# A two-layer encoder step on one core: the second layer's up product in seven block products for 26 of its 32 units, with the residual stored to DRAM and loaded again in between

## The chip, the cores and the metric

The kernel runs on one core of a Trainium2 chip. The metric is the device time of one execution in microseconds; smaller is better. The kernel before took 2478.04 us, the median of 3 runs (2475.95 to 2481.3).

## What is computed

The reference is one inference step of a two-layer encoder on 1024 prompt rows and 32 sample rows (T = 1056 columns when the rows are laid along the free axis), width D = 1024, fp32. Layer 0 is an mLSTM mixer and an MLP, layer 1 is a chunk-band attention and an MLP. Only the MLP of layer 1 matters here:

```python
u = x * (1 + sc2) + sh2                       # x: after the first LayerNorm of the layer
f = jnp.square(jax.nn.relu(u @ w_up)) @ w_down   # 1024 -> 4096 -> 1024
x = layer_norm(ALPHA * x + (1 + g2) * f, ln_g, ln_b)
```

Results must hold fp32 accuracy, so every fp32 operand of these products is split into a high part (a cast to fp32r) and a low part (the rest), and each product is three matmuls: high x high, high x low, low x high.

## The kernel before, in words

**Tiles.** Feature rows lie on the 128 partitions, the 1056 columns on the free axis. `QN` = 264 columns are a quarter; two quarters are a pair. Pair 1 (columns 528 to 1055) goes first (`tp0` = 1), pair 0 second (`tp1` = 0). The 4096 hidden rows are 16 blocks `pb` of 256 rows. A *unit* is one block for one pair, so there are 32. The modulated input lies in `u2[pair]` (high and low, 8 row blocks of 128), and the residual x in one tile `ACC` (128 x 8 x 1056 fp32) from the pool `acc1` (L1705), into which the down product adds.

**Up product** (`mlp7`, L1124). `up_tile` (through `up_mm` and `proj`, L118 to L120) makes one 128 x 264 tile with 8 row blocks x 3 = 24 matmuls; a unit has four of them, 96 matmuls. ScalarE applies relu from PSUM (L1159) and the square (L1162) in a tile `H`. VectorE then forms sums and differences of the four quadrants (L1164 to L1166), splits them into `HL`, and one store puts the seven forms of the unit into DRAM (`hd`, L1170). Blocks 14 and 15 (`NW` = 14 and up) go through `up_plain` (L1180) and are stored as plain high and low parts (`hpl`, L1191). The weights of a block come in two loads of 512 KB (`up_weights`, `wblock`, `split` at L89 on ScalarE and L90 on VectorE).

**Down product.** Blocks 0 to 13 lie in four groups (`GRP`: 3, 4, 3, 4 blocks). For each group and each of four column blocks of `w_down`, `unit` (L1268) makes a product in Strassen's manner with seven block products (`PRODS`) where eight stand in the plain one. `forms` (L1222) makes the seven forms of the weights: 7 splits, each a ScalarE cast and a VectorE subtraction, and 4 VectorE sums or differences. Each of a unit's products is kg x 3 matmuls (kg blocks in the group) for each pair and is added to `ACC` by VectorE (L986). `Rooms` (L1098) hands out free space in SBUF, and `fill` (L1261) loads the wanted forms from `hd` into it (`fx`, L1117), pair 1 before pair 0, in the order of `PRODS`. The first column block of the first group goes first for pair 1 and then for pair 0. Last come blocks 14 and 15 as a plain product (`hs` from `hpl`).

**Order of the work.** PE's order in the down product is written out by hand (`manual_schedule`). All other instructions of an engine stand in a fixed list that the scheduler makes when the kernel is built; each engine runs its list in order and stops at the first instruction whose inputs are not there. All loads and stores are issued by one queue, SP's, in the order of its list. `Flow` spreads long tasks such as the LayerNorm (`norm`, L846) over the product's ticks: `L.ready(i)` ends the LayerNorm of the i-th column block (order 2, 1, 0). When the up product begins, the LayerNorm of blocks 1 and 0 is still running beside it.

**Buffers.** Raw weights go through a ring `raw` of 3 tiles, split weights and forms through a ring `wc` of 6, `H` has 3 tiles and `HL` one.

Of the kernel before, what the change touches and what calls it, by code (L numbers as in the profile page):

```python
# [75 lines left out]
def trunk_kernel(ctx: ExitStack, tc: tile.TileContext, a, o):  # L76
# [61 lines left out]
    xsp = [dr.tile([P, KC, T], F32, name=f"xsp{l}") for l in range(2)]  # L138
# [954 lines left out]
    B11, B22, B21, T1, T3, T2, T4 = range(7)  # L1093
# [30 lines left out]
    def mlp7(L):  # L1124
# [5 lines left out]


        l, mm = L.l, L.alloc
        w_dn = a["w_down"][l]
        hd = [[dr.tile([7, P, kg, 2, QN], F32, name=f"hd{l}_{g}_{tp}") for tp in range(2)]
              for g, (_, kg) in enumerate(GRP)]
        hpl = dr.tile([4, P, 2, T], F32, name=f"hpl{l}")
        hh_cm = tc.tile_pool(name=f"hh{l}", bufs=1, reuse_waits="tile")
# [13 lines left out]

        def up_tile(pb, f, q):

            tp = q // 2
            ps = up_mm(pb, f, q)
            if (pb, tp) not in hts:
                hts[pb, tp] = [hhp.tile([P, 8, QN], F32, tag="H", name=f"H{l}_{pb}_{tp}", bufs=3), 0]
            H = hts[pb, tp][0]
            nc.scalar.activation(H[:, ((0, 1), (3, 2))[f][q % 2]], ps, AF.Relu)  # L1159
            hts[pb, tp][1] += 1  # L1160
            if hts[pb, tp][1] == 4:
                nc.scalar.activation(H[:, 0:4], H[:, 0:4], AF.Square)  # L1162
                HL = hhp.tile([P, 7, 2, QN], F32R, tag="HL", name=f"HL{l}_{pb}_{tp}", bufs=1)
                nc.vector.tensor_sub(H[:, 4:6], H[:, 1:3], H[:, 0:2])  # L1164
                nc.vector.tensor_sub(H[:, 6], H[:, 2], H[:, 4])
                nc.vector.tensor_sub(H[:, 7], H[:, 3], H[:, 6])  # L1166
                split(HL[:, 0, 0], HL[:, 0, 1], H[:, 0])
                split(HL[:, 1:, 0], HL[:, 1:, 1], H[:, 2:])
                g = [i for i, (p0, kg) in enumerate(GRP) if p0 <= pb][-1]
                nc.sync.dma_start(hd[g][tp][:, :, pb - GRP[g][0]].rearrange("f p l t -> p f (l t)"),  # L1170
                                  HL.bitcast(F32).rearrange("p f l t -> p f (l t)"))
            flow.tick(QN / 96)
# [7 lines left out]
        def up_plain(pb, tp):  # L1180
            for f in range(2):
                r = tmp_t([P, 2, QN], f"hr{l}_{pb}_{f}_{tp}")
                for i in range(2):
                    nc.scalar.activation(r[:, i], up_mm(pb, f, 2 * tp + i), AF.Relu)
                    flow.tick(QN / 96)
                nc.scalar.activation(r, r, AF.Square)
                name = f"hl{l}_{pb}_{f}_{tp}"
                hl = hlp.tile([P, 2, 2, QN], F32R, tag="hl", name=name, bufs=2) if pb == NPB - 1 else \
                    ring.tile([P, 2, 2, QN], F32R, tag="raw", name=name, bufs=3)
                split(hl[:, 0], hl[:, 1], r)  # L1190
                nc.sync.dma_start(hpl[2 * (pb - NW) + f, :, :, 2 * tp * QN:2 * (tp + 1) * QN],  # L1191
                                  hl.bitcast(F32).rearrange("p l q t -> p l (q t)"))

        tp0, tp1 = L.pairs

        for i in range(2):
            L.ready(i)
            for pb in range(3):
                for f in range(2):
                    up_tile(pb, f, L.quarters[i])  # L1200
                if i and pb < 2:
                    del wups[pb]
                    up_w(3 + pb)
        up_unit(3, tp0)
        up_unit(4, tp0)
        L.ready(2)
        for pb in (2, 3, 4, 0, 1):
            up_unit(pb, tp1)
        for pb in range(5, NW):
            for tp in L.pairs:  # L1210
                up_unit(pb, tp)
        for pb in range(NW, NPB):
            up_w(pb)
        hh_cm.__exit__(None, None, None)
        f4_cm = tc.tile_pool(name=f"f4{l}", bufs=1, reuse_waits="tile")
        f4p = f4_cm.__enter__()
        f4 = [f4p.tile([P, KG, 2, QN], F32R, tag=f"f4{i}", name=f"fx_4{i}_{l}") for i in range(4)]
        hl_cm = tc.tile_pool(name=f"hl{l}", bufs=1, reuse_waits="tile")
        hlp = hl_cm.__enter__()


        def forms(g, m, nm):  # L1222

            raw = []
            p0, kg = GRP[g]
            for i in range(2):
                r = raw_tile([P, kg, 256], f"rdn_{nm}_{i}")
                nc.sync.dma_start(r, w_dn[p0 * 256:(p0 + kg) * 256, m * 256:(m + 1) * 256].rearrange(
                    "(k s p) c -> s p k c", s=2, p=P)[i])
# [24 lines left out]
            w = pair()  # L1254
            split(w[:, 0, 0], w[:, 0, 1], a22)
            yield out

        fx, nfx = {}, {}
        want = []
# [31 lines left out]
        order_f = [f for _, f, _, _, _ in PRODS]  # L1291
        preps, got = {}, {}
        units = [(g, m, [(tp0,), (tp1,)] if g + m == 0 else [(tp0, tp1)]) for g in range(len(GRP)) for m in range(4)]

        def prep(i):
            if i < len(units):
                preps[i] = forms(*units[i][:2], f"{l}_{i}")
                next(preps[i])
        for t in f4:
            rooms.add(t)  # L1300
        want += [(tp, f) for tp in L.pairs for f in order_f]
        fill(0, fx)
        for tp in L.pairs:
            up_plain(NW, tp)
        prep(0)
        up_plain(NW + 1, tp0)
# [3 lines left out]
        for t in L.rooms(tp0):  # L1310
            rooms.add(t)
        fill(0, fx)
        up_plain(NW + 1, tp1)
        for t in L.rooms(tp1):
            rooms.add(t)
        fill(0, fx)
        hl_cm.__exit__(None, None, None)
        f5_cm = tc.tile_pool(name=f"f5{l}", bufs=1, reuse_waits="tile")
        rooms.add(f5_cm.__enter__().tile([P, KG, 2, QN], F32R, name=f"fx_5_{l}"))
        fill(0, fx)  # L1320
        with tc.manual_schedule(engines={mybir.EngineType.PE}):
            for i, (g, m, phases) in enumerate(units):
                more = g + 1 < len(GRP)
                if i == 1:
                    rooms.add(ring.tile([P, KG, 2, QN], F32R, tag="wc", name=f"fx_w{l}", bufs=6))
                if m == 1 and more:
# [4 lines left out]
                def step(j):  # L1331
                    if i + 1 in preps and j in (0, 1, 3, 5):
                        got[i + 1] = next(preps[i + 1])
                    if j == 3:
                        prep(i + 2)
# [5 lines left out]
                unit(g, m, phases, got[i], step, after)  # L1341
                if m == 3:
                    assert not want
                    fx, nfx = nfx, {}
# [14 lines left out]
        f5_cm.__exit__(None, None, None)  # L1359
        f4_cm.__exit__(None, None, None)  # L1360

# [344 lines left out]
    ACC = acc_cm1.__enter__().tile([P, KC, T], F32, name="ACC")  # L1706
# [28 lines left out]
    def end_out1(ti):  # L1735
        norms[ti] = flow.add(norm(ti, 2, f"n10_{ti}", W10[ti == rev[-1]]), now=NOW)
        qo_cm[ti].__exit__(None, None, None)
        if ti == 1:
            open_u2(0)
# [4 lines left out]
    wup1 = {}  # L1744

    def early_up(ti, pr):

        if ti == rev[-1] and pr:
            wup1[pr - 1] = up_weights(1, pr - 1)
# [3 lines left out]
    class L1:  # L1753
# [3 lines left out]
        pairs, quarters = (1, 0), (3, 2, 1, 0)  # L1757

# [3 lines left out]
        def ready(i):  # L1762
            flow.finish(norms[rev[i]])

# [65 lines left out]
```

## Time and profile before

| what | value |
|---|---|
| median of 3 runs | 2478.04 us (2475.95 to 2481.3) |
| span of the profiled execution, first to last instruction | 2476.9 us |
| PE busy / weight loads / VectorE / ScalarE, share of the span | 98% / 94% / 71% / 41% |
| up product of layer 1, first to last matmul start | 1730.4 to 2108.3 us, 3072 matmuls |
| down product of layer 1 | 2108.3 us to the end of the span |
| hd stores in layer 1 | 28 of 1848 KB |

The profile is one execution on the chip. Times are from the span's start. "Busy" is time in which an engine works on at least one instruction; matmuls overlap each other, so the rate is read as matmuls per us and not from the length of one. In a list of groups, each row is a source line, an engine and an operation, output <- inputs, then the count, the busy time with the mean length of one in ns, and the idle time ahead with what ended it. In a timeline the first two numbers are start and length.

### The profile page before, as it was taken

To read this page: it belongs to the slowest core of one execution; us is meant where nothing else is said; L and a number is where in the kernel's file an instruction comes from. 1 tells how busy PE (TensorE), PEld (TensorE's weight loads), DVE (VectorE), ACT (ScalarE), POOL (GpSimd) and SP (SyncE) were. 2 spreads that over 40 slices of the span, in tenths; PEclk is the share of its full clock that TensorE was granted. 3 is DMA by queue.
4 is the path that set the end of the run, shared out by engine and by line. 5 is a ranking of instruction groups with operands and counts; after the bars stand their busy time and mean duration, and the time that the engine had idled before them with its cause. 6 is when DMAs were issued, how large, how long until landed. Compare 5 with 4: busy or idle time off the path is not lost.

```text
span 2476.9 us, 42628 instructions
## 1 busy us (share of the span) xinstructions
PE 2419.5 (98%) x16844; PEld 2328.9 (94%) x16844; DVE 1753.2 (71%) x3974; ACT 1021.7 (41%) x2118; POOL 167.1 (7%) x315
## 2 busy tenths in 40 slices
PE   7999999999999999999999999999999999999997
PEld 4999999999999999999999977789999999899997
DVE  4899999788679679677597666746853442776758
ACT  4554456382212212212266566754754443221212
POOL 0211100000000000000001134410000000000003
PEclk9999999999999999999999989999999999999999
DMA  8433233313224224224122310051475547767632
GB/s 297 122 108 96 83 93 108 131 35 111 79 92 131 84 91 130 83 89 149 43 85 91 92 44 2 18 147 31 136 249 214 210 179 259 259 237 274 255 129 71
DMA packets 236220, 318.10 MB, mean 128 GB/s; under 512 B 11624, under 2 KB 185084, under 8 KB 234996
## 3 DMA queue, kind: packets, MB, share of 16 engines
q1 hardware_dynamic: 236020, 315.38, 38.4%
q8 instruction: 132, 2.16, 0.4%
q14 instruction: 68, 0.56, 0.1%
HBM read 242.79 MB, written 74.91 MB: 128 GB/s over the span
## 4 chain that ended last, share of the span: by engine, by line
PE 81%; DVE 6%; DMA 6%; ACT 2%; issue 1%; POOL 0%; SPq 0%; ACTq 0%; DVEq 0%; POOLq 0%
PE up L118 10%; PE up L120 10%; PE up L119 10%; PE dn L1283 9%; PE dn L119 5%; PE dn L118 5%; PE dn L120 5%; DMA fx<-hd 3%; PE pv L1616 3%; PE s L1559 2%; PE pt L1594 2%; PE o L118 1%; PE o L119 1%; PE o L120 1%; PE qk L118 1%; PE qk L120 1%
## 5 line engine op out<-in xcount | busy, mean ns | idle before, releaser
L120 PE MATMUL up<-u,w_up 128*128 128x264 f32 x1024 | 293.0, 286 | 0.0
L118 PE MATMUL up<-u,w_up 128*128 128x264 f32 x1024 | 292.4, 286 | 0.0
L119 PE MATMUL up<-u,w_up 128*128 128x264 f32 x1024 | 291.2, 284 | 0.0
L1283 PE MATMUL dn<-fx,wf 128*128 128x264 f32 x2208 | 275.7, 286 | 7.4 <-DMA fx<-hd 6.3
L1283 PEld LDWEIGHTS dn<-fx,wf 128*128 128x128 f32 x2208 | 272.4, 189 | 9.6 <-issue 4.6
L119 PE MATMUL dn<-h,w_dn 128*128 128x384 f32 (+1 forms) x768 | 249.5, 325 | 0.0
L118 PE MATMUL up<-U,w_up 128*128 128x384 f32 (+1 forms) x768 | 249.2, 324 | 0.0
L119 PE MATMUL up<-U,w_up 128*128 128x384 f32 (+1 forms) x768 | 247.9, 323 | 0.0
L118 PE MATMUL dn<-h,w_dn 128*128 128x384 f32 (+1 forms) x768 | 247.8, 323 | 0.0
L120 PE MATMUL up<-U,w_up 128*128 128x384 f32 (+1 forms) x768 | 247.6, 322 | 0.0
L120 PE MATMUL dn<-h,w_dn 128*128 128x384 f32 (+1 forms) x768 | 247.3, 322 | 0.0
L119 PEld LDWEIGHTS up<-u,w_up 128*128 128x128 f32 x1024 | 193.9, 189 | 0.0
L118 PEld LDWEIGHTS up<-u,w_up 128*128 128x128 f32 x1024 | 193.8, 189 | 0.0
L120 PEld LDWEIGHTS up<-u,w_up 128*128 128x128 f32 x1024 | 193.4, 189 | 0.0
L986 DVE SCALAR_TENSOR_TENSOR ACC<-dn,ada,ACC 128x264 f32<-128x264 f32 (+4 forms) x328 | 132.0, 427 | 86.0 <-PE dn L1283 73.6
L238 DVE SCALAR_TENSOR_TENSOR aacc<-rada,cs,aacc 128x256 f32<-128x256 f32 x448 | 190.4, 478 | 0.0
L986 DVE SCALAR_TENSOR_TENSOR acc<-dn,ada,acc 128x384 f32<-128x384 f32 (+2 forms) x256 | 119.5, 487 | 47.7 <-PE dn L120 46.2
L1025 ACT ACTIVATE r<-up 128x384 f32<-128x384 f32 (+1 forms) x96 | 44.3, 463 | 246.9 <-PE up L120 236.9
L119 PEld LDWEIGHTS dn<-h,w_dn 128*128 128x128 f32 x768 | 144.5, 188 | 0.2 <-DVE h L1028 0.2
L120 PEld LDWEIGHTS dn<-h,w_dn 128*128 128x128 f32 x768 | 144.5, 188 | 0.0
L120 PEld LDWEIGHTS up<-U,w_up 128*128 128x128 f32 x768 | 144.3, 188 | 0.0
L118 PEld LDWEIGHTS up<-U,w_up 128*128 128x128 f32 x768 | 144.2, 188 | 0.1
(354 smaller groups left out, 6001.5 us busy)
## 6 DMA issues: line engine op xcount, KB each, us to landing
hd<-HL SPq DMA_DIRECT2D x28, 1848.0 KB
raw_up<-in_w_up_dram SPq DMA_DIRECT2D x68, 512.0 KB
rada<-in_w_ada_dram SPq DMA_DIRECT2D x64, 512.0 KB
fx<-hd SPq DMA_DIRECT2D x37, 528.0 KB
raw_dn<-in_w_down_dram SPq DMA_DIRECT2D x36, 512.0 KB
ada_room<-in_w_ada_dram SPq DMA_DIRECT2D x32, 512.0 KB
fx<-hd SPq DMA_DIRECT2D x50, 264.0 KB
fx<-hd SPq DMA_DIRECT2D x16, 792.0 KB
```

The source lines that it names most:

```text
L118: nc.tensor.matmul(ps, wh, mov(0, k), start=(k == 0), stop=False)
L119: nc.tensor.matmul(ps, wh, mov(1, k), start=False, stop=False)
L120: nc.tensor.matmul(ps, wl, mov(0, k), start=False, stop=(k == nk - 1))
L238: nc.vector.scalar_tensor_tensor(acc[:, cnd], raw[:, k], sc, acc[:, cnd], op0=ALU.mult, op1=ALU.add)
L986: nc.vector.scalar_tensor_tensor(xs, ps[:, off + o:off + o + mm_], gate[:, fc, cnd:cnd + 1], xs, op0=ALU.mult, op1=ALU.add)
L1025: nc.scalar.activation(r, ps[:, :n], AF.Relu)
L1283: nc.tensor.matmul(p, ws[w][:, wl, k], t[:, s0, xl], start=first and k + n_ == 0, stop=k == kg - 1 and n_ == 2, skip_group_check=not first)
L1559: nc.tensor.matmul(s[:, b, :w], qst, kk[i][:, g, k0 + j0:k0 + j0 + w], start=(i == 0), stop=(i == 1))
L1594: nc.tensor.transpose(pt[:kp, j - j0, pr * P:(pr + 1) * P], ps_[pr][:, j * P:j * P + kp], ident)
L1616: nc.tensor.matmul(pv[64 * e:64 * e + 64, :nq], V[:kp, vt0 + j, g * 64:(g + 1) * 64], pts[e][:kp, j, :nq], start=(j == 0), stop=(j == nt - 1))
```

## The change

The first six blocks that the up product takes (`FIRST`: 10 to 15) are done as before, but for pair 1 alone. The other 26 units (pair 1 of blocks 0 to 9, pair 0 of all sixteen) go through the new class `Seven`: 7 products of 4 x 3 matmuls, 84 in place of 96. Three things are needed for that.

- *Forms of the input* (`tforms`, once for each pair): differences of the four quarters of `u2`. Two of them go to the tile `TF`, one to a tile `ext` (pair 1) or a tile of the ring `wc` (pair 0), and one replaces a quarter of `u2` itself. `TF` takes the place of `ACC`: each column block of `ACC` is stored to DRAM when its LayerNorm ends, and `reload` brings the residual back (four loads of 1056 KB) when the last product has read `TF`.
- *Forms of the up weights*: `forms`, now for up and down weights alike, one set per block. The sequence of weight sets runs on from the up into the down product, always one set ahead.
- *Other evictions*: partial sums are copied by ScalarE or added by VectorE into `H`, and relu follows on three quarters at once. `h_forms` now splits into two tiles, `HL` (4 forms) and `HM` (3 forms), with a store each, so that `H` has 6 parts and not 8. Blocks 14 and 15 are stored from `HL` in four parts each.

Two units are interleaved on PE: products of one unit stand between those of the next. The space for the first group's forms is given free in three steps: `ext` and pair 1's `u2` after the last unit of pair 1, then, after the last unit, four tiles in the place of `H`, `HL` and `HM`, and pair 0's `u2`. `up_plain` and its four plain units, which stood between the up and the down product, are gone.

```diff
+        def h_forms(pb, tp, H):
+            nc.scalar.activation(H[:, 0:4], H[:, 0:4], AF.Square)
+            hl = hhp.tile([P, 4, 2, QN], F32R, tag="HL", name=f"HL{l}_{pb}_{tp}", bufs=1)
...
+            nc.vector.tensor_sub(H[:, 4:6], H[:, 0:3:2], bass.AP(H.tensor, H[:, 1].offset, [H.ap[0], [-QN, 2], [1, QN]]))
+            split(hl[:, :, 0], hl[:, :, 1], H[:, 1:5])
+            nc.sync.dma_start(dst[:, 0:4], hl.bitcast(F32).rearrange("p f l t -> p f (l t)"))
+            nc.vector.tensor_sub(H[:, 1], H[:, 2], H[:, 4])
+            nc.vector.tensor_sub(H[:, 3], H[:, 3], H[:, 1])
+            hm = hhp.tile([P, 3, 2, QN], F32R, tag="HM", name=f"HM{l}_{pb}_{tp}", bufs=1)
+            split(hm[:, :, 0], hm[:, :, 1], H[:, 1:6:2])
+            nc.sync.dma_start(dst[:, 4:7], hm.bitcast(F32).rearrange("p f l t -> p f (l t)"))
...
+        def tforms(tp, ext):
...
+            def less(t, x, y):
+                nc.vector.tensor_sub(t, x[0].bitcast(F32), y)
+                nc.vector.tensor_add(t, t, x[1].bitcast(F32))
+
+            def diff(t, x, y):
+                less(t, x, y[0].bitcast(F32))
+                nc.vector.tensor_sub(t, t, y[1].bitcast(F32))
+            t3 = raw(3)
+            diff(t3, b(B22), b(B12))
+            yield
+            split(ext[:, 0], ext[:, 1], t3)
+            yield
+            t1 = raw(1)
+            diff(t1, b(B12), b(B11))
+            yield
+            split(TF[tp, 0][0], TF[tp, 0][1], t1)
+            less(t1, b(B22), t1)
+            yield
+            split(TF[tp, 1][0], TF[tp, 1][1], t1)
+            less(t1, b(B21), t1)
+            yield
+            split(*b(B12), t1)
...
+        class Seven:
...
+                for k in range(4):
+                    for n_, (wl, xl) in enumerate(((0, 0), (0, 1), (1, 0))):
+                        nc.tensor.matmul(p, self.ws[w][:, wl, k], moving(f, tp, xl, k), start=first and k + n_ == 0,
+                                         stop=k == 3 and n_ == 2, skip_group_check=not first)
+                if i in (0, 2, 3):
+                    nc.scalar.copy(H[:, {0: 4, 2: 5, 3: 2}[i]], p)
+                elif i in (1, 4, 5):
+                    o_, x = {1: (1, 4), 4: (2, 2), 5: (0, 5)}[i]
+                    nc.vector.tensor_add(H[:, o_], p, H[:, x])
+                    if i == 5:
+                        nc.scalar.activation(H[:, 0:3], H[:, 0:3], AF.Relu)
+                else:
+                    nc.scalar.activation(H[:, 3], p, AF.Relu)
+                    h_forms(pb, tp, H)
...
+            for _, j, i in sorted((7 * j + 2 * i, j, i) for j in range(len(jobs)) for i in range(7)):
...
+                sevens[j].product(i)
+                if tp == seq[n][1][-1]:
+                    advance(n, i)
+                if j == lone - 1 and i == 6:
+                    rooms.add(ep.tile([P, KG, 2, QN], F32R, tag="e", name=f"fx_e{l}"))
+                    for t in L.rooms(tp0):
+                        rooms.add(t)
+                    fill(0, fx)
+        L.reload()
...
+        seq = [(pb, (0,) if pb > 9 else (1, 0) if pb else (0, 1)) for pb in (0, 1, 2, 14, 3, 4, 5, 15, 6, 7, 8, 10, 9, 11,
+                                                                             12, 13)]
...
+        def reload():
+            x = acc["all"] = accp.tile([P, KC, T], F32, tag="acc", name="ACC2")
+            for k in range(0, KC, 2):
+                nc.sync.dma_start(x[:, k:k + 2], xsp[2][:, k:k + 2])
```

More of the change, by code (lines that the diff above doesn't have):

```diff
@@ L1178, in up_unit @@
                         up_tile(pb, f, q)
[L1180 to L1222, printed above, removed]
+        def tforms(tp, ext):
+            def b(i):
+                kap, q = {B11: (0, 0), B12: (0, 1), B21: (1, 0), B22: (1, 1)}[i]
+                return [L.u4(hl, tp, kap, q) for hl in range(2)]
+            def raw(i):
+                return raw_tile([P, 4, QN], f"t{i}_{l}_{tp}")
+            def less(t, x, y):
[19 more added lines that the diff above has]
+            split(*b(B12), t1)
@@ new lines, in mlp7 @@
+        tp0, tp1 = L.pairs
+        TF = {}
+        for i in range(2):
+            L.ready(i)
+            for j, pb in enumerate(L.first[:3]):
+                for f in range(2):
+                    up_tile(pb, f, L.quarters[i])
+                if i and j < 2:
+                    del wups[pb]
+                    up_w(L.first[3 + j])
+        exts[tp0] = ep.tile([P, 2, KG, QN], F32R, tag="e", name=f"ext_{l}")
+        tf = tforms(tp0, exts[tp0])
+        next(tf)
+        next(tf)
+        rest = L.first[3:]
```

158 lines of the change are left out of this document (107 added, 51 removed).

## The prediction

> **What bounds the kernel now.** I read the page's span and engine lines first, then the busy times by stage, then the instructions that touch the tile `up`.
>
> ```profile
> span 2476.9 us, 42628 instructions
> PE 2419.5 (98%) x16844; PEld 2328.9 (94%) x16844; DVE 1753.2 (71%) x3974; ACT 1021.7 (41%) x2118; POOL 167.1 (7%) x315
> ```
>
> TensorE is busy nearly everywhere. By stage (length, busy us of PE, weight loads, VectorE, ScalarE, POOL, then clock, DMA share, GB/s):
>
> ```profile
> 1730.00:1800.00 70.00, 69.62 (x552) 69.41 (x553) 58.23 (x100) 52.85 (x93) 0.00 (x0) 0.98 0.43 142
> 1800.00:2108.00 308.00, 308.00 (x2525) 308.00 (x2524) 128.08 (x160) 141.38 (x223) 0.00 (x0) 1.00 0.63 222
> 2108.00:2140.00 32.00, 26.13 (x187) 24.86 (x187) 20.13 (x47) 8.91 (x19) 0.00 (x0) 0.89 0.96 363
> L118 PE MATMUL up<-u,w_up x1024: 280/285/422, 1730.4 to 2108.1; 128*128 128x264 f32 x171
> ```
>
> The second row is PE without a gap: 308 us / 2525 = 0.122 us per matmul. That is the pace; the 285 ns in the last row is the length of one, three of which overlap. VectorE has much room there (128 of 308 us), but little in the first row (58 of 70): the LayerNorm of the layer runs beside the first tiles. The third row is the entry of the down product: 187 matmuls where 32 us hold 262, so 75 x 0.122 = 9.2 us are lost, to these waits:
>
> ```profile
> 2118.26 1.73 PE L1283 MATMUL dn<-fx,wf 128*128 128x264 f32 x12 [0.60 <-DMA fx<-hd]
> 2121.57 1.00 PE L1283 MATMUL dn<-fx,wf 128*128 128x264 f32 x6 [1.58 <-DMA fx<-hd]
> 2125.74 2.32 PE L1283 MATMUL dn<-fx,wf 128*128 128x264 f32 x9 [3.17 <-DMA fx<-hd]
> ```
>
> So PE sets the end in the up product, loads at the entry of the down product, and VectorE is the next engine where the up product begins.
>
> **The change, part by part.** The VectorE and ScalarE prices (mean ns of one behind the comma) are:
>
> ```profile
> L986 DVE SCALAR_TENSOR_TENSOR ACC<-dn,ada,ACC 128x264 f32<-128x264 f32 x160 | 78.4, 490 | 61.9 <-PE dn L1283 60.9
> L90 DVE TENSOR_TENSOR HL<-H,HL 128x1584 fp32r<-128x1584 f32 x28 | 50.6, 1807 | 12.7 <-ACT HL L89 12.5
> L90 DVE TENSOR_TENSOR w_up<-raw_up,w_up 128x1024 fp32r<-128x1024 f32 x36 | 44.1, 1224 | 64.9 <-ACT w_up L89 64.9
> L90 DVE TENSOR_TENSOR wf<-s,wf 128x512 fp32r<-128x512 f32 x32 | 20.6, 687 | 1.6 <-ACT wf L89 1.6
> L1164 DVE TENSOR_TENSOR H<-H 128x528 f32<-128x528 f32 x28 | 19.7, 705 | 70.5 <-ACT H L1162 70.5
> L1166 DVE TENSOR_TENSOR H<-H 128x264 f32<-128x264 f32 x28 | 12.1, 432 | 0.9
> L896 DVE TENSOR_TENSOR ACC<-ACC,w_n 128x768 f32<-128x768 f32 x8 | 7.4, 953 | 0.1
> L841 DVE TENSOR_SCALAR ut_n<-ACC,comb 128x384 f32<-128x384 f32 x16 | 6.9, 474 | 0.0
> L844 DVE TENSOR_TENSOR u<-ut_n,u 128x384 fp32r<-128x384 f32 x8 | 4.2, 552 | 0.0
> L1159 ACT ACTIVATE H<-up 128x264 f32<-128x264 f32 x112 | 43.3, 388 | 127.2 <-PE up L120 127.0
> L1162 ACT ACTIVATE H<-H 128x1056 f32<-128x1056 f32 x28 | 30.4, 1086 | 0.3
> ```
>
> From 1024 columns (1224) to 1584 (1807) a column costs 1.04 ns, so an operation on 1056 columns takes 1.257 us and one on 792 about 0.97.
>
> *(a) Matmuls gone.* 26 units x 12 = 312; 312 x 0.122 = **-38.1 us**. A unit of seven products takes 84 x 0.122 = 10.25 us, all 26 take 266.5.
>
> *(b) The forms of the input.* The first six blocks, now for pair 1 alone, are 576 matmuls or 70.3 us: PE has done them by 1801.7 (1730.4 + 70.3, with six LayerNorm matmuls). The first unit of seven needs pair 0's forms and its weights' forms. In VectorE's list both kernels are alike up to one instruction of the last LayerNorm:
>
> ```profile
> 1727.84 1.22 DVE L90 TENSOR_TENSOR w_up<-raw_up,w_up 128x1024 fp32r<-128x1024 f32 x1
> 1728.98 0.55 DVE L884 TENSOR_TENSOR q_n<-q_n 128x384 f32<-128x384 f32 x1
> 1759.89 0.55 DVE L884 TENSOR_TENSOR q_n<-q_n 128x384 f32<-128x384 f32 x1
> ```
>
> From the last row's instruction on to the split of the third weight form, without which product 2 can't start, the changed list holds 86: 34 of 1056 columns (28 input forms, 6 of `HL`) 42.7 us; 4 of 1024, 4.9; 4 of 792, 3.9; 4 of 768, 3.8; 4 of 528, 2.8; 7 of 512, 4.8; 21 of 384, 10.8; 8 of 264, 3.4. Sum 77.1. The next one starts up to 0.08 us before the last ends (first two rows: 1.22 long, 1.14 apart), but not where it needs its result; over the stretch from 1722.8 to 1759.9, where the list is known in both, the gain was 0.054 each, so 72.5: VectorE gets there at 1832.4. The writes into `TF` also wait for the last third of `ACC` (1.57 MB) to be stored, about 2 us more: 1834.4. PE could have started product 2 at 1801.7 + 24 x 0.122 = 1804.6. **+30 us**, and nothing covers it, since PE's list goes on with just these products. Between: 25 (0.08 everywhere, no store wait) and 36 (lengths in full, the wait).
>
> *(c) The run of seven-product units.* A block with two units needs of VectorE 11 operations of 512 columns, 11 of 264, 2 each of 528, 792 and 1056: 18.2 us, or 16.6 with the overlap, in 20.5 us of PE. The sums out of PSUM have no row; the nearest are 0.432 (no PSUM) and 0.490 (L986, PSUM and a scalar), and I take 0.43; the difference is 0.3 us a block and hidden. [...] ScalarE has 15 of 20.5 us (7 casts of about 0.62, and for a unit 4 evictions at 0.39, a square of 1.09 and about 2.7 for the other relu and the casts). A bank is used again only four products later, so an eviction has about 4 us. Some waits for the ring of three raw tiles and at VectorE's long operations: **+4 us**, between 0 and 12.
>
> *(d) The last three blocks.* 11, 12 and 13 have one unit each: 7.6 us of weight forms and 5.3 for `H`, 11.8 with the overlap, in 10.25 us. VectorE's list also puts block 11's five `H` operations, about 5.8 us with their casts between, ahead of block 13's weight forms, whose first product stands next on PE 1.5 us after block 11's last one. **+8 us**, between 3 and 10.
>
> *(e) The entry of the down product.* Let U be the end of the up product. Pair 1's seventh form and all seven of pair 0 go into the place of `H`, `HL` and `HM`, free when block 13's last split is done. In VectorE's list that split stands behind 23 others (eleven are sums into `ACC`), 12 us of work from about U + 3: U + 15. SP's list puts these loads behind the store of `HM` and the last quarter of the reload, so 0.8 + 1.1 + 0.27 MB go first, then seven forms of 0.81 MB.
>
> ```profile
> GB/s 0 0 326 382 380 349 288 401 420 427 400 260 374 373 395 381 102 153 360 416 427 429 331 402 392 410 429 420 395 364 350 411 399 108 144 395 250 228 103 356
> DMA packets 10490, 24.25 MB, mean 323 GB/s; under 512 B 704, under 2 KB 4288, under 8 KB 10485
> 1729.13 1.97 SPq L96 DMA_DIRECT2D raw_up<-in_w_up_dram  x2
> 1732.90 1.05 ACT L89 CAST w_up<-raw_up 128x1024 fp32r<-128x1024 f32 x1
> ```
>
> The first two rows are 2075 to 2150 us of the kernel before: the queue gives up to 400 GB/s. A load's data is used some 3.5 us after its issue (last two rows). So 5.4 + 14.2 + 3 us: the last form is there at U + 37.5 and its product ends at U + 38.6. Unhindered, the 126 matmuls would end at U + 15.4; 23 us are lost, 9.2 were lost before: **+14 us**, between 8.5 (430 GB/s, no latency) and 18 (323 GB/s). The reload's first quarter (1.1 MB) is issued when the last product has read `TF`, 4 to 5 us before U, and lands about U, just in time. The 4.3 MB stored beside the LayerNorm meet an almost idle queue.
>
> **Sum:** -38.1 + 30 + 4 + 8 + 14 = +17.9 us. The sum stands against the profiled span, 2476.9; the median is 1.1 above it, and I add the same to it: 2478.0 + 17.9 = **2496 us**, slower by 0.7%.
>
> **Rivals.**
> *PE stays the bound.* If the input's forms were ready when PE is and the entry were as before, only (a) would be left: 2440 us. For it: 94% weight loads on the page, and VectorE busy in 186 of 378 us over both rows of the up product. Against it: it needs (b)'s 72.5 us of list to fit into the 42 us up to 1801.7. [...] 5%.
> *A clean tail.* (b) and (c) as forecast, but blocks 11 to 13 and the entry cost no more than now, because single units draw on weight forms made ahead, and the loads into `H`'s place start with U: -38.1 + 30 + 4 = -4: 2474. It decides from the point where block 13's splits come before U + 5. The list speaks against it. 13%.
> *VectorE bounds the whole run.* Of 16.6 us in 20.5, four more per block in waits (for raw tiles, which are three for two per block, or for a cast) use up the room; each further us costs PE one. With 2 us for each of 16 blocks, 32 in place of 4 in (c): 2524. For it: lists that alternate between two engines, as L90 waiting 64.9 us for its cast in the rows above. Against it: the down product has the same weight forms and runs at full pace. 17%.
> *The change doesn't do what it says:* all 312 matmuls are gone from PE's list, so no.
>
> **How the numbers follow.** The forecast gets 65%, with 2483 to 2513 as its own range. The low ends of (b) to (e) give -38.1 + 25 + 0 + 3 + 8.5 = -1.6: 2476; the high ends -38.1 + 36 + 12 + 10 + 18 = +38: 2516. With part of both outer rivals, 2474 to 2518. Faster by more than 0.2% (about what a measurement of this kernel can tell from no change: 5 us): the first rival and a part of the second, 10%; within 0.2%, 2473 to 2483: the rest of the second and the forecast's lower edge, 13%; slower 77%.
>
> **What would show it.** (a) 312 fewer matmuls with 0.122 us between them where PE runs. (b) PE idle between about 1800 and 1834, in part before block 15's first tile, released by VectorE; VectorE without a gap from 1723 to 1835. (c) small gaps only. (d) a gap of 5 to 8 us before block 13's first product. (e) PE waiting some 20 us for `fx` behind the up product. Wrong if VectorE has gaps before 1830 and PE none, if gaps come with every block, or if the `fx` loads into `H`'s place start within a few us of U.

## The result, and the profile after

The changed kernel takes 2491.79 us (median of 4 runs, 2486.63 to 2492.83), the kernel before 2479.67 us beside it: a ratio of 1.0053, 95% interval 1.0034 to 1.0073. It is slower by 12 us by the medians, 13 by the ratio, though 312 matmuls are gone. The forecast was 2496 us, 18 us slower.

The page of the changed kernel, its first lines:

```profile
span 2484.8 us, 42567 instructions
PE 2386.1 (96%) x16532; PEld 2293.4 (92%) x16532; DVE 1888.6 (76%) x4228; ACT 1081.7 (44%) x2232; POOL 167.3 (7%) x315
```

PE does 33 us less work in a longer span, and VectorE 135 us more. The span is only 7.9 us longer than before, for a reason that isn't the change: this execution began the up product at 1725.0 us, the one of before at 1730.4, and the code up to there differs in little more than the stores of the residual (the kernels of the experiments, with nearly the code of the changed one up to there, began it between 1726.2 and 1731.3). From the first matmul of the up product to the end it is 759.8 us after and 746.5 before: **+13.3 us**, close to what the medians and the ratio say. All that follows is read within that stretch.

Busy times by stage after (length, then PE, weight loads, VectorE, ScalarE, POOL with their instructions, the granted clock, the DMA share, GB/s):

```profile
1725.00:1787.00 62.00, 61.76 (x491) 61.54 (x491) 61.00 (x101) 50.94 (x86) 0.00 (x0) 0.97 0.52 177
1787.00:1832.00 45.00, 26.02 (x140) 24.13 (x139) 41.21 (x45) 21.40 (x33) 0.00 (x0) 0.66 0.53 174
1832.00:2077.00 245.00, 245.00 (x2015) 245.00 (x2014) 197.47 (x331) 164.96 (x283) 0.00 (x0) 1.00 0.70 242
2077.00:2103.00 26.00, 17.90 (x127) 17.39 (x127) 19.44 (x34) 15.15 (x27) 0.00 (x0) 0.80 0.75 264
2103.00:2145.00 42.00, 23.98 (x163) 22.10 (x162) 21.39 (x47) 9.70 (x16) 0.00 (x0) 0.80 1.02 389
```

and, of the kernel before, the entry of the down product in as many us:

```profile
2108.00:2150.00 42.00, 36.13 (x269) 34.86 (x269) 28.81 (x68) 10.35 (x22) 0.00 (x0) 0.92 0.91 339
```

The third row gives the pace: 245.00 / 2015 = 0.1216 us for a matmul. What a stage lasts beyond its matmuls at that pace is lost there:

| stage | us | matmuls | at 0.1216 | lost | lost before |
|---|---|---|---|---|---|
| block 15's tiles and the first units of seven | 45.0 | 140 | 17.0 | 28.0 | 0 |
| run of units of seven | 245.0 | 2015 | 245.0 | 0 | 0 |
| last blocks | 26.0 | 127 | 15.4 | 10.6 | 0 |
| entry of the down product | 42.0 | 163 | 19.8 | 22.2 | 9.3 |

28.0 + 10.6 + 12.9 - 312 x 0.1216 = +13.6, so the table holds the whole difference. PE's waits in these stretches, from its timeline (start, length, instruction, in brackets the idle time ahead and what ended it):

```profile
1790.95 0.59 PE L120 MATMUL up<-u,w_up 128*128 128x264 f32 x1 [3.39 <-DVE w_up L90]
1812.44 0.81 PE L1297 MATMUL up<-u,wf_u 128*128 128x264 f32 x2 [7.73 <-ACT wf_u L89]
1817.02 2.57 PE L1297 MATMUL up<-u,wf_u 128*128 128x264 f32 x10 [3.77 <-DVE wf_u L90]
1820.52 3.30 PE L1297 MATMUL up<-u,wf_u 128*128 128x264 f32 x12 [0.94 <-ACT wf_u L89]
1825.81 0.81 PE L1297 MATMUL up<-TF,wf_u 128*128 128x264 f32 x2 [1.99 <-ACT wf_u L89]
1827.78 4.50 PE L1297 MATMUL up<-TF,wf_u 128*128 128x264 f32 x22 [1.17 <-DVE wf_u L90]
...
2085.54 0.81 PE L1297 MATMUL up<-u,wf_u 128*128 128x264 f32 x2 [7.81 <-ACT wf_u L89]
...
2125.96 1.03 PE L1375 MATMUL dn<-fx,wf_d 128*128 128x264 f32 x3 [12.85 <-DMA fx<-hd]
```

Six waits around the first unit, one ahead of block 13, one long one for the forms of the down product, and none in the run of 245 us. In the stretch of 45 us PE is idle for 19.0 of the 28.0 us lost; the other 9.0 are matmuls at a slower pace, of which the last section has more.

### The profile page after: what moved, and what is told of

Read it like the earlier page. It is cut to its first block, busy times and chain, and to the rows that moved or that the text cites. A ratio compares the mean times of both kernels' runs of the same rounds, so it can differ in the third digit from the quotient of the medians.

```text
span 2484.8 us, 42567 instructions
## 1 busy us (share of the span) xinstructions
PE 2386.1 (96%) x16532; PEld 2293.4 (92%) x16532; DVE 1888.6 (76%) x4228; ACT 1081.7 (44%) x2232; POOL 167.3 (7%) x315
## 4 chain that ended last, share of the span: by engine, by line
PE 77%; DVE 10%; DMA 4%; ACT 2%; issue 1%; POOL 0%; SPq 0%; DVEq 0%; ACTq 0%; POOLq 0%
PE up L1297 10%; PE dn L1375 10%; PE up L118 5%; PE up L120 5%; PE up L119 5%; PE dn L119 5%; PE dn L118 5%; PE dn L120 5%; PE pv L1719 3%; PE s L1662 2%; PE pt L1697 2%; DMA fx<-hd 2%; PE op_a L118 1%; PE op_a L119 1%; PE op_a L120 1%
## 5 line engine op out<-in xcount | busy, mean ns | idle before, releaser
L1375 PE MATMUL dn<-fx,wf_d 128*128 128x264 f32 x2016 | 256.1, 286 | 19.4 <-DMA fx<-hd 16.4
L1375 PEld LDWEIGHTS dn<-fx,wf_d 128*128 128x128 f32 x2016 | 250.5, 190 | 22.0 <-DMA fx<-hd 15.0
L1297 PE MATMUL up<-u,wf_u 128*128 128x264 f32 x1248 | 169.5, 289 | 20.5 <-ACT wf_u L89 16.5
L1297 PEld LDWEIGHTS up<-u,wf_u 128*128 128x128 f32 x1248 | 160.3, 192 | 22.1 <-ACT wf_u L89 17.2
L119 PEld LDWEIGHTS dn<-h,w_dn 128*128 128x128 f32 x768 | 144.5, 188 | 0.2 <-DVE h L1028 0.2
L120 PEld LDWEIGHTS dn<-h,w_dn 128*128 128x128 f32 x768 | 144.5, 188 | 0.0
L120 PEld LDWEIGHTS up<-U,w_up 128*128 128x128 f32 x768 | 144.3, 188 | 0.0
L118 PEld LDWEIGHTS up<-U,w_up 128*128 128x128 f32 x768 | 144.2, 188 | 0.1
L119 PEld LDWEIGHTS up<-U,w_up 128*128 128x128 f32 x768 | 144.2, 188 | 0.0
L118 PEld LDWEIGHTS dn<-h,w_dn 128*128 128x128 f32 x768 | 143.9, 187 | 0.2
L1027 DVE TENSOR_TENSOR r<-r 128x384 f32<-128x384 f32 (+1 forms) x96 | 50.0, 522 | 102.7 <-ACT h L1026 102.2
L89 ACT CAST w_up<-raw_up 128x1024 fp32r<-128x1024 f32 x44 | 46.0, 1047 | 134.6 <-DMA raw_up<-in_w_up_dram 105.8
```

The lines of the kernel that those rows point to most:

```text
L89: nc.scalar.copy(dst_h, src)
L118: nc.tensor.matmul(ps, wh, mov(0, k), start=(k == 0), stop=False)
L119: nc.tensor.matmul(ps, wh, mov(1, k), start=False, stop=False)
L120: nc.tensor.matmul(ps, wl, mov(0, k), start=False, stop=(k == nk - 1))
L1027: nc.vector.tensor_mul(r, r, r)
L1297: nc.tensor.matmul(p, self.ws[w][:, wl, k], moving(f, tp, xl, k), start=first and k + n_ == 0, stop=k == 3 and n_ == 2, skip_group_check=n ...
```

## The experiments

All ratios are to the kernel before on the same chip. The changed kernel's is 1.0053, so 0.004 of ratio is 10 us.

**Fewer operations for the input's forms** (`nolow`).

```diff
             def less(t, x, y):
                 nc.vector.tensor_sub(t, x[0].bitcast(F32), y)
-                nc.vector.tensor_add(t, t, x[1].bitcast(F32))
...
                 less(t, x, y[0].bitcast(F32))
-                nc.vector.tensor_sub(t, t, y[1].bitcast(F32))
```

> Left out: in the forms of the input, the additions and subtractions of the low parts (12 of the 28 VectorE operations of 1056 columns), so the output is not the reference's. Theory (VectorE's list is what PE waits for ahead of the first seven-product units): 12 x 1.17 us = 14 us less of list; PE's idle time between the last plain tiles and the steady run falls from 19 us to 5 to 9, and the kernel is 10 to 14 us faster than the changed one, that is within 4 us of the kernel before. Rival (loads and casts of the weight forms set it, and VectorE only fills its time): idle stays above 15 us and the kernel within 4 us of the changed one.

Measured: 1.0002 (0.9991 to 1.0014). The stretch of 45 us in its profile:

```profile
1789.00:1834.00 45.00, 35.64 (x255) 34.68 (x255) 38.46 (x50) 26.94 (x41) 0.00 (x0) 0.85 0.59 196
```

255 matmuls instead of 140, 14.0 us less lost: just the 12 x 1.17 us that VectorE no longer does. PE's idle time fell to 9.4 us, a little above the 5 to 9 expected, and from the first up matmul to the end it is 747.1 us, 12.7 less. VectorE's list is what PE waits for there; the rival falls.

**More cover in front** (`plain8b`).

```diff
-                for n in ((), (0,), (0, 1), (0, 1), (1, 1), (1, 0, 1))[2 * j + f]:
+                for n in ((), (), (1,), (1,), (1, 1), (1, 1), (0,), (0,), (0,), (0,))[2 * j + f]:
...
-    FIRST = [10, 11, 12, 13, 14, 15]
+    FIRST = [8, 9, 10, 11, 12, 13, 14, 15]
...
+        seq = [(pb, (0,) if pb > 7 else (1, 0) if pb else (0, 1)) for pb in (0, 1, 14, 2, 8, 3, 15, 4, 9, 5, 6, 10, 7, 11,
+                                                                             12, 13)]
```

The edit does one thing more than the expectation says: as the first two lines show, all forms of pair 0's input are now made ahead of the rest of pair 1's.

> Eight plain blocks for pair 1 ahead of the seven-product units in place of six. PE gets 2 x 96 matmuls = 23.4 us more work there and 24 matmuls = 2.9 us more in all; VectorE gets 12.5 us more (two weight splits and H's forms for each block). Theory (the stall is missing cover): the idle time there falls from 19 us to 8 or less, and the kernel is about 8 us faster than the changed one (between 3 and 20). Rival (VectorE bounds the whole up product): the stall only moves to later units, and the kernel is within 3 us of the changed one or slower by the 2.9.

Measured: 1.0049 (1.0034 to 1.0064), no clear difference from the changed kernel; by this the rival stands as well. Only the profile tells them apart. There the stretch from the first up matmul to the end is 755.3 us, 4.5 less than the changed kernel's. The loss around the first unit, by 363 matmuls in 62 us, is 17.9 us and not 28.0; idle there is 11.0 + 1.4, not 19.0, and the run of units of seven behind it has no gap, so the stall did not move to later units. 10.1 us less lost there, 2.9 us for the 24 added matmuls, and 2 to 3 us more lost later, at block 13, at the entry and behind it, leave the 4.5. The sign and the place are the theory's, the size about half of it. How much of it is cover and how much the order of the forms was not separated.

**Which space, or which place in the queue** (`swap`, `tail`).

```diff
# swap: pair 0's input is handed out ahead of the place of H, HL and HM
-        for i in range(4):
-            rooms.add(f4p.tile([P, KG, 2, QN], F32R, tag=f"f4{i}", name=f"fx_4{i}_{l}"))
         for t in L.rooms(tp1):
             rooms.add(t)
+        for i in range(4):
+            rooms.add(f4p.tile([P, KG, 2, QN], F32R, tag=f"f4{i}", name=f"fx_4{i}_{l}"))
# tail: the same, and called behind the last product's matmuls, ahead of its h_forms
+        def leave():
+            L.reload(0, 2)
+            for t in L.rooms(tp1):
+                rooms.add(t)
+            fill(0, fx)
```

> The space for the last seven forms of the first group is handed out from pair 0's input first and from the place of H, HL and HM last. All else, and the place of the loads in SP's list behind the store of HM_13 and the last quarter of the reload, stays. Theory (the loads stand behind that store in the queue's list): no change, within 3 us of the changed kernel, and the loads again start about 14 us behind the last up matmul. Rival (the space is what they wait for): they start within 5 us of it, and the kernel is 8 to 10 us faster than the changed one.

Measured: 1.0071 (1.0056 to 1.0086). SP's timeline shows the loads where they were:

```profile
2123.30 0.36 SPq L1174 DMA_DIRECT2D hd<-HM  x1
2123.70 0.49 SPq L1885 DMA_DIRECT2D ACC<-xsp  x1
2124.30 12.36 SPq L1117 DMA_DIRECT2D fx<-hd  x11
```

They start 15.2 us behind the first `dn` matmul (2109.1), directly behind the store of `HM` and the reload. From the first up matmul to the end it is 761.5 us, 1.7 more than the changed kernel's, and the intervals of the two ratios overlap. Space that is handed out earlier gives nothing.

> Pair 0's input is handed out first, and these loads are issued behind the first quarter of the reload and ahead of the last unit's forms; the other three quarters of the reload come behind the loads. Theory (queue order and space make the stall at the entry of the down product): the loads start within 3 us of the last up matmul, PE's wait for fx falls from 16 us to about 5, and the kernel is 8 to 12 us faster than the changed one. Rival (the queue's throughput sets it: 4.3 MB of reload and 5.7 MB of forms at 400 GB/s are 25 us whatever their order): the wait stays above 12 us, gain 0 to 3 us.

Measured: 1.0070 (1.0055 to 1.0085), no faster than the changed kernel. The first of the loads goes out 0.5 us behind the first `dn` matmul (2107.7), the next seven 5.9 us behind it, after a store of `HM`, and yet little is won. The entry in its profile:

```profile
2108.21 0.45 SPq L1117 DMA_DIRECT2D fx<-hd  x1
2113.24 0.36 SPq L1174 DMA_DIRECT2D hd<-HM  x1
2113.65 4.31 SPq L1117 DMA_DIRECT2D fx<-hd  x7
...
2107.70:2149.70 42.00, 26.51 (x184) 24.62 (x183) 20.72 (x46) 8.83 (x14) 0.00 (x0) 0.84 1.01 379
...
2128.36 1.77 PE L1377 MATMUL dn<-fx,wf_d 128*128 128x264 f32 x9 [1.95 <-DMA fx<-hd]
2139.01 1.22 PE L1377 MATMUL dn<-fx,wf_d 128*128 128x264 f32 x4 [8.88 <-DMA fx<-hd]
```

184 matmuls instead of 163, 2.6 us. The wait of 12.9 us has become smaller ones and one of 8.9 at the last form. With 379 GB/s and a DMA share of 1.01 over the whole window the DMA engines are full, as they were in the changed kernel (389 GB/s, 1.02). That speaks for the rival: the entry is bound by bytes. What my theory expected, 8 to 12 us, did not come; from the first up matmul to the end it is 757.7 us, 2.1 less.

**The sums and differences on an idle engine** (`pool1`).

```diff
         def tforms(tp, ext):
+            eng = nc.gpsimd if tp == tp0 else nc.vector
...
-                nc.vector.tensor_sub(t, x[0].bitcast(F32), y)
+                eng.tensor_sub(t, x[0].bitcast(F32), y)
```

> Ten of the 28 VectorE operations of 1056 columns that make the input's forms (the sums and differences for pair 1) go to POOL, which is idle there; the splits stay. Theory (VectorE's list holds the first seven-product units): 10 x 1.17 = 11.7 us less of list, the idle time there falls from 19 us to about 8, and the kernel is 9 to 12 us faster than the changed one. POOL's own ten take about 23 us, by its 2.26 us for 1024 columns elsewhere in this kernel, and fit beside. Rival (POOL is too slow, or slows VectorE while both run): VectorE's operations of 1056 columns grow beyond 1.25 us or the splits wait for POOL, and the gain is under 4 us.

Measured: 1.0114 (1.0099 to 1.0129), about 15 us slower than the changed kernel. The rival's mechanism came, with a loss that neither expectation had. From VectorE's, POOL's and ScalarE's timelines:

```profile
1765.61 3.42 POOL L1208 TENSOR_TENSOR t<-u 128x1056 f32<-128x1056 f32 x1 [1.16 <-DVE w_up L90]
1769.10 3.32 POOL L1209 TENSOR_TENSOR t<-t,u 128x1056 f32<-128x1056 f32 x1
```

```profile
1766.62 3.48 DVE L90 TENSOR_TENSOR w_up<-raw_up,w_up 128x1024 fp32r<-128x1024 f32 x1
1770.03 2.69 DVE L1170 TENSOR_TENSOR H<-H 128x264 f32<-128x264 f32 x1
...
1820.30 1.07 ACT L89 CAST TF<-t 128x1056 fp32r<-128x1056 f32 x1 [5.74 <-POOL t L1209]
1821.40 1.26 DVE L90 TENSOR_TENSOR TF<-t,TF 128x1056 fp32r<-128x1056 f32 x1 [3.40 <-ACT TF L89]
```

A VectorE operation on 264 columns that takes 0.43 us alone takes 2.69 while POOL works. The ten operations of POOL take 2.55 to 4.53 us each. Nine VectorE operations are longer by 2.2 to 2.3 us each, 20 us together, where VectorE saves 10 x 1.17 = 11.7 us. Another 3.4 us come from the last two rows: POOL's operations hang on each other, ScalarE's cast waits 5.74 us for them, and VectorE waits for the cast. That is 12 of the 15.7 us by which the stretch from the first up matmul to the end grew (775.5 us).

**The order of the blocks** (`ord2`).

```diff
-        seq = [(pb, (0,) if pb > 9 else (1, 0) if pb else (0, 1)) for pb in (0, 1, 2, 14, 3, 4, 5, 15, 6, 7, 8, 10, 9, 11,
-                                                                             12, 13)]
+        seq = [(pb, (0,) if pb > 9 else (1, 0) if pb else (0, 1)) for pb in (0, 1, 2, 11, 3, 4, 12, 5, 6, 10, 7, 8, 13, 9,
+                                                                             14, 15)]
```

> Another order of the blocks: 11, 12 and 13 go between the blocks with two units, and 14 and 15, whose units make no sums or differences and no HM, are the last. Theory (ScalarE's cast into the one HL tile waits for the store of the unit before, and the casts of the next block's weights stand behind it): the gap of 7.8 us ahead of the last block's first product falls to 4 or less, and the entry of the down product loses 2 to 4 us less since HM_13 no longer stands ahead of its loads; 5 to 11 us faster than the changed kernel. Rival (a block with one unit lacks time on VectorE whatever its place): gaps of 2 to 4 us appear at each of the moved blocks, gain 0 to 3 us.

Measured: 1.0034 (1.0021 to 1.0047). From the first up matmul to the end it is 754.2 us, 5.6 less than the changed kernel's. No gap appears at the moved blocks, nor ahead of the last block's first product. A new one stands ahead of the down product, whose first matmuls come here before the last 12 of the up product:

```profile
2099.12 1.18 PE L1375 MATMUL dn<-fx_e,wf_d 128*128 128x264 f32 x3 [4.75 <-ACT wf_d L89]
```

ScalarE had waited 1.86 us for the load of that weight block, which SP issues behind the loads of pair 1's forms and two stores. So the theory holds for the gap, and part of the gain is taken back by the queue. (Up to the first `dn` matmul it is 370.5 us, where the changed kernel has 378.0, but that leaves out the 12 matmuls behind it. The 7.5 us that the expectation of `best2` takes for the up product are this difference, and too many.)

**All three** (`best1`), **and without POOL** (`best2`). In these, and in `best3`, `best4` and `best6`, the last three quarters of the reload are called for only behind pair 0's second product of the first down unit.

> The three edits together: pair 1's sums and differences of the input on POOL, blocks 14 and 15 last, the loads behind the up product issued ahead of the last unit's forms with three quarters of the reload behind them. If the three losses add up: 11 + 7 + 3 = about 21 us faster than the changed kernel, that is 6 to 10 us faster than the kernel before (0.996 to 0.998 of it). Rival (the queue's throughput at the entry takes back what is won ahead of it): within 5 us of the kernel before.

Measured: 1.0065 (1.0048 to 1.0082). Both expectations missed, since both had counted a gain from POOL, and its loss is in it.

> As the kernel with all three edits, but with pair 1's sums and differences back on VectorE: blocks 14 and 15 last, and the loads behind the up product ahead of the last unit's forms. If what the two edits gave in the profiles adds up (7.5 us in the up product, 2.2 to 2.7 behind it): 10 us faster than the changed kernel, 3 us slower than before (1.000 to 1.002 of it). Rival (the queue gives back at the entry what the order wins): as the kernel with the order alone, 1.0034.

Measured: 1.0028 (1.0017 to 1.0039). First up matmul to the end: 748.5 us, 11.3 less than the changed kernel's; by the runs it lies between the two expectations. Against `ord2` the stretch is 5.7 us shorter, so in this order of the blocks the order of the loads does count by the profiles; by the runs the two cannot be told apart.

**PE kept busy in the gaps** (`warm`).

```diff
+        WARM = {(0, 0): 95, (0, 2): 25}
...
+                if (j, i) in WARM:
+                    pw = mm(f"warm{j}_{i}")
+                    for _ in range(WARM[j, i]):
+                        nc.tensor.matmul(pw[:, :QN], ones_d, L.u4(0, tp0, 0, 0)[:, 0], start=True, stop=True)
                 sevens[j].product(i)
```

> 120 matmuls that no one reads (a constant times pair 1's input) stand in the two larger gaps of PE ahead of and in the first seven-product units: 95 ahead of the first product, 25 ahead of the third. Theory (matmuls after a gap run at half the pace because the granted clock falls when PE is idle, 0.52 there): with the gaps filled the clock stays over 0.9 and a product of 12 matmuls takes 1.5 to 1.7 us there and not 2.6 to 3.3; since the products wait for VectorE's list all the same, the kernel gains only 0 to 3 us. Rival (the pace is set by the operands that come late or by what VectorE and the DMAs do at that time): the products still take over 2.4 us.

Measured: 1.0051 (1.0036 to 1.0066); first up matmul to the end 759.1 us, 0.7 less.

```profile
1806.29 8.80 PE L1415 MATMUL warm<-u,ones_d 128*128 128x264 f32 x72
1814.95 0.51 PE L1297 MATMUL up<-u,wf_u 128*128 128x264 f32 x2
1819.52 2.57 PE L1297 MATMUL up<-u,wf_u 128*128 128x264 f32 x10 [4.05 <-DVE wf_u L90]
1823.23 3.29 PE L1297 MATMUL up<-u,wf_u 128*128 128x264 f32 x12 [1.15 <-ACT wf_u L89]
1826.32 4.62 PE L1415 MATMUL warm<-u,ones_d 128*128 128x264 f32 x25
1830.78 3.08 PE L1297 MATMUL up<-TF,wf_u 128*128 128x264 f32 x24
```

Of the 95, 23 were placed ahead of block 15's tiles. Where PE had been fed without a gap, 24 matmuls take 3.08 us (last row), 4.50 for 22 in the changed kernel. A gap of 4.05 us was left within the first product, and behind it 12 matmuls take 3.29 us, as slow as before (3.30); the granted clock is 0.74 from 1812 to 1832, where the changed kernel has 0.52. So here the pace went with PE's idle time, as the theory has it, but the clock did not stay over 0.9: two of the products still take 2.6 and 3.3 us.

The slow pace did cost something on the way. The steady run begins 104.0 us behind the first up matmul, 107.1 in the changed kernel, and the last up matmul comes 375.1 us behind it, 377.8 there. Most of these 3 us are gone again by the end, where only 0.7 are left.

**Ten plain blocks, and the queue's order** (`best4`, `best3`, `best6`). All three keep the order with 14 and 15 last and the early loads; `best4` has eight plain blocks, `best3` and `best6` ten. In all kernels with more plain blocks pair 0's input forms are made ahead of pair 1's.

```diff
+    FIRST = [6, 7, 8, 9, 10, 11, 12, 13, 14, 15]
...
+        seq = [(pb, (0,) if pb > 5 else (1, 0) if pb else (0, 1)) for pb in (0, 6, 1, 7, 2, 8, 9, 3, 10, 11, 4, 12, 13, 5,
+                                                                             14, 15)]
...
# best6 alone: the loads of pair 1's forms are called for eight products (a little over a unit) later
-                    fill(0, fx)
+                if (j, i) == (lone + 1, 3):
+                    fill(0, fx)
```

> The same with eight plain blocks in front and the units of blocks 8 to 13 between the blocks with two units: the 6.5 us that eight plain blocks gave in the up product come on top: 3 to 4 us faster than before (0.9985). Rival (eight blocks with one unit instead of six overload VectorE in the steady run, gaps there): no better than with six plain blocks.

Measured: 0.9998 (0.9988 to 1.0008), 2474.20 us where `best2` has 2482.37 on the same chip: better than with six plain blocks, so the rival falls, but no different from the kernel before, where 3 to 4 us less were expected.

> The same with ten plain blocks in front, 22 seven-product units. Cover grows by 23.4 us of matmuls for 12.5 us of VectorE, 2.9 us more matmuls in all. Theory (missing cover): idle time ahead of the first seven-product units falls from 12 us with eight plain blocks to 5 or less, 3 to 6 us faster than with eight: 0.997 of the kernel before. Rival (VectorE's list grows with the plain blocks as well): the idle time stays near 10 us, and the kernel is 0 to 3 us slower than with eight.

Measured: 0.9987 (0.9977 to 0.9998), 2472.59 us: 1.6 less than with eight plain blocks, where 3 to 6 were expected. The stall ahead of the first units of seven is gone, as the theory has it, and a new one stands at the end:

```profile
PE up L1297 <- ACT wf_u L89: 11.5, 1, 11.5
PE dn L1377 <- DMA fx<-hd: 10.6, 5, 6.3
PE up L118 <- ACT w_up L89: 5.1, 2, 2.8
...
2079.06 0.62 ACT L89 CAST wf_u<-rdn_u 128x512 fp32r<-128x512 f32 x1 [8.27 <-DMA rdn_u<-in_w_up_dram]
```

The first three rows are PE's waits from the start of the up product into the down product (us, times, longest). The first is block 15: ScalarE waits 8.3 us (last row) for the second half of its weights, which SP issued directly behind a row of loads of forms.

> As the kernel with ten plain blocks, but the loads of pair 1's forms for the down product are issued only when the weights of block 15 and of the first down unit have been called for. In the kernel with ten plain blocks PE waits 11.5 us ahead of block 15: ScalarE's cast waits for the second half of block 15's weights, which stood in SP's list behind seven loads of forms. Theory: that gap falls to 2 or less and the forms, 5 MB or 13 us of the queue, still land in time: 8 to 11 us faster, 0.995 to 0.996 of the kernel before. Rival (the queue has no room left there, so the wait moves to the first products of the down product): 0 to 3 us faster, 0.998 to 0.999.

Measured: **0.9960** (0.9945 to 0.9975), 2466.34 us against 2475.22: the fastest of all, faster than the kernel before. The same waits, and one of ScalarE's:

```profile
PE dn L1377 <- DVE ACC L986: 14.0, 1, 14.0
PE dn L1377 <- DMA fx<-hd: 4.6, 1, 4.6
PE up L118 <- ACT w_up L89: 4.2, 2, 2.4
...
2090.09 1.07 ACT L89 CAST HL<-H 128x1056 fp32r<-128x1056 f32 x1 [7.29 <-DMA hpl<-HL]
```

The wait ahead of block 15 is gone; the up product lasts 354.2 us, 378.0 before and after the change. At the entry a wait of 14.0 us has taken the place of several: VectorE's additions stand behind a split that waits for ScalarE's cast into `HL`, and that cast waits 7.29 us for the store of block 14's `HL`. Theory and rival are both right, one for each end, and the sum is the theory's.

## Why the prediction was right

The direction, the places of the losses and the sum held. In (b), (d) and (e) the step behind the number was only partly right, and in (b) two errors cancelled. The terms, one by one:

**(a)** 312 x 0.1216 = 37.9 us; the forecast had 38.1.

**(b)** Forecast 30 us, lost 28.0. The forecast had VectorE at the third weight form's split at 1832.4 to 1834.4; less the 5.4 us by which this execution came earlier, 1827.0 to 1829.0.

```profile
1826.44 0.68 DVE L1264 TENSOR_TENSOR s_u<-rdn_u,s_u 128x512 f32<-128x512 f32 x1
1827.04 2.49 DVE L90 TENSOR_TENSOR wf_u<-s_u,wf_u 128x512 fp32r<-128x512 f32 x4
1829.45 0.68 DVE L90 TENSOR_TENSOR wf_u<-rdn_u,wf_u 128x512 fp32r<-128x512 f32 x1
```

The split begins at 1827.04, and PE goes on at 1827.78. That 14 us of it hang on 12 operations, `nolow` has shown. The list of 86 instructions is as forecast, and it took 72.55 us (1754.49 to 1827.04), where 72.5 were forecast. That it fits so well is luck: VectorE stood idle for 3.1 us in it, so the list itself took only 69.4. The overlap was 0.08 us for each instruction and not 0.054, the lengths came to 1 us less, and waits that the forecast did not name filled the difference. The 2 us that it did name, for the store of `ACC`, are not among them:

```profile
1796.19 0.39 ACT L1183 ACTIVATE H<-up 128x264 f32<-128x264 f32 x1 [4.07 <-PE up L120]
1797.57 1.26 DVE L90 TENSOR_TENSOR TF<-t,TF 128x1056 fp32r<-128x1056 f32 x1 [1.97 <-ACT TF L89]
```

VectorE waits 1.97 us for ScalarE's cast into `TF`. That cast stood behind an eviction that waited 4.07 us for PE, which had waited for block 15's weights and then ran the tile at half pace; the store had been issued 8.7 us before the cast. In `warm`, where that tile ran at full pace, this gap is not there.

**(c)** Forecast 4 (0 to 12), measured 0. VectorE is busy 197.5 of 245 us, on average 16.5 in 20.5, and 16.9 over the two-unit blocks 6 to 8 (50.5 in 61.4 us), where 16.6 were forecast. (The forecast counted eleven operations of 264 columns for such a block; the kernel has ten, 0.4 us less.) The waits that were added on top don't reach PE. The rival in which VectorE bounds the whole run is refuted by the third stage row. The sums out of PSUM took 0.42 to 0.43 us (78 of them, 0.425 on average), as taken.

**(d)** Forecast 8 (3 to 10), lost 10.6, just above. PE's idle time is 8.1 us of this, as forecast; the other 2.5 are matmuls at a slower pace (10 in 2.57 us, and a granted clock of 0.53 from 2085.5 to 2091.0), which the forecast left out. The place was right, the step behind the gap only in part: it named the length of VectorE's list. ScalarE's timeline shows another holder.

```profile
2077.76 0.38 ACT L1300 COPY H<-up 128x264 f32<-128x264 f32 x1
2080.78 1.07 ACT L89 CAST HL<-H 128x1056 fp32r<-128x1056 f32 x1 [2.64 <-DMA hd<-HL]
2084.11 0.85 ACT L89 CAST HM<-H 128x792 fp32r<-128x792 f32 x1 [2.26 <-DVE H L1171]
2084.87 1.28 ACT L89 CAST wf_u<-rdn_u 128x512 fp32r<-128x512 f32 x2
```

There is one `HL` tile, so its cast waits 2.64 us for the store of the unit before, and the casts of block 13's weights stand behind it in ScalarE's list. VectorE was idle for 3.3 us meanwhile. The next 2.26 us ScalarE waits for VectorE's sums, which are among the five operations that the forecast named. `ord2`, where the last blocks have lighter units, lost the gap, which fits both causes. A second `HL` tile would have been the direct test and wasn't tried, so the share of each stays open.

**(e)** Forecast 14 (8.5 to 18), measured 12.9. With U at 2103.0 the loads were forecast from U + 15 and the last form at U + 37.5; the loads begin at 2117.6, U + 14.6, and PE's last wait for `fx` ends at 2139.9, U + 36.9.

```profile
2116.68 0.36 SPq L1174 DMA_DIRECT2D hd<-HM  x1
2117.08 0.49 SPq L1885 DMA_DIRECT2D ACC<-xsp  x1
2117.61 12.55 SPq L1117 DMA_DIRECT2D fx<-hd  x11
```

`swap` and `tail` show what of the explanation counts. The freed space alone does nothing (`swap`). Block 13's last split sets the start as forecast, but through the store of `HM` that waits for it and stands ahead of the loads in SP's list. And when some of the loads start early (`tail`), bytes at 379 to 389 GB/s set nearly the same end. The forecast's sum was by bytes and came out; the place "free when block 13's last split is done" was not what the loads waited for.

So the forecast change was 4.3 us too much by the profiles: 4 from (c), 2 from (b), 1 from (e), less 2.6 from (d). Of the rivals, the clean tail (2474) fell to (d) and (e), and that PE stays the bound (2440) to (b). The weight loads stood at 94% before and stand at 92% now, in a kernel with 1.9% fewer matmuls and 0.5% more time. That the bound passes to other engines from stage to stage is what decided here.

## What to carry to other kernels

A cut in an engine's work pays only where that engine is the one waited for: add up, stage by stage, what the other engines have to do before it can start the cheaper work, from their own instruction lists. Put the old, self-sufficient work in front as cover until those lists have been worked off, and put blocks with light ends last. In a single in-order queue look at what stands ahead of each load that is needed soon, and count the bytes at the queue's rate before reordering it.

## What the runs showed of the hardware

**VectorE's operations took longer beside POOL's.** 264 columns take 2.69 us beside POOL and 0.43 alone (`pool1`); beside nine of POOL's ten operations on 1056 columns one VectorE operation each was 2.2 to 2.3 us longer than alone, whether on 264 columns or on 1056. I had expected POOL to run beside.

**Behind some of PE's waits the matmuls ran at half the pace.** Behind the wait of 3.39 us the matmuls of block 15's tiles start 0.22 us apart until 1797.05, and 0.1216 in the steady run; the granted clock is 0.50 from 1790.4 to 1797.1 and 1.00 in the steady run. Full pace came back after 6.1 us of matmuls. In the kernel before, around a wait of 3.17 us behind two shorter ones (rows of the prediction), the granted clock is 0.50 from 2124.0 to 2130.6. I had left this out. Around the first unit it cost 3 us by `warm`, most of which was lost again by the end; ahead of block 13 it is 2.5 of the 10.6 us lost.
